# A two-block transformer kernel: one wide matmul for both parts of the tokens in products with stationary weights

## The chip, the cores and the metric

The kernel runs on one core of a Trainium2 chip. The metric is the device time of one execution in microseconds (us); lower is better. The kernel before was timed in three runs.

## The reference, cut to what matters

Two transformer blocks over 256 tokens of width 1024, in fp32. The first has four mixers (gated delta rule, spatial gating, sliding window, memory) on slices of one large input product, each weighted by a gate:

```python
h = _rmsnorm(x, norm_pre)
cols = h @ w_in
...
proj = jnp.einsum("btnc,ncd->btnd", ys, w_up)
gates = jax.nn.sigmoid(gate_logits.reshape(B, T, N_BRANCH, D))
merged = jnp.sum(gates * proj, axis=2)
out = merged @ w_out
return x + _rmsnorm(out, norm_post)
```

The second part has two layers, each with a feed-forward net, an attention (MLA in one, NSA in the other) and a second feed-forward net:

```python
def swiglu(x, w_gate, w_up, w_down):
    return (jax.nn.silu(x @ w_gate) * (x @ w_up)) @ w_down
```

## The kernel before, in words

All large products are made in fp32 accuracy from three products of halves: each operand is split into a part `h` (rounded to the format that TensorE multiplies, fp32r) and a remainder `l`, and `h h + h l + l h` is summed in a PSUM bank. `mm3` (lines 226 to 232) issues these three matmuls; after each it calls `drip`, which issues one or two steps of other work (transposes, attention, the delta rule).

**Weights.** `unit` (lines 192 to 213) brings up to 128 x 2048 numbers by a DMA from SP's queue into `raw` (two buffers) and splits them in two halves of 1024 columns: ACT casts `raw` to `wh` (line 210), DVE subtracts and writes `wl` (line 211). `wh` and `wl` have four buffers each, so units are made some three ahead, and a new unit waits for TensorE to leave the buffer of the fourth before it.

**Tokens.** `xpair` and `ypair` (lines 363 to 371) make the transposed, split tokens: two tiles `xTh` and `xTl` (or `yTh`, `yTl`), each of [128, 8 or 4 k tiles, 256 tokens].

**Two kinds of product.** In one kind (`Product`, line 240) the tokens are stationary and 512 columns of weights stream past. In the other, `ws` (lines 289 to 301), a 128 x 128 block of weights is stationary and the 256 tokens stream; the result has channels on the partitions. `ws` walks over blocks of 128 channels (`j`); two blocks share a bank of `acc` (two banks), and `evac` is called once per bank with 512 columns:

```python
pv = acc().rearrange("p (j t) -> p j t", j=2)
for j in range(2):
    js = slice(j1 + j * P, j1 + (j + 1) * P)
    for k in range(nk):
        ...
        mm3(pv[:, j, :], h[:, k, js], l[:, k, js], xh, xl, k == 0, k == nk - 1)
evac((j0 + j1) // P, 2, pv)
```

So one pair (block, k tile) costs three weight loads and three matmuls of 256 columns. `ws` makes, with 8 k tiles: the three parts of the convolution's input (`convolve`, line 568, whose copy of the bank at line 575 has a raised priority), the gates of two branches (`z_ws`), `qs`, `xq` and `mkT` (lines 846 to 936), the merge gates (line 1006), the queries of NSA (line 1479), and in each of the four feed-forward nets the gate and up products of `hidden` (lines 1078 to 1091), one unit of 256 channels at a time, 18 units per net. With 4 k tiles it makes the up-projections `w_up` of the merge (line 1020), 8 units of 512 channels.

Evacuation reads the bank directly: `silu2` is a tanh on ACT (line 413) and a combining operation on DVE (line 414); `ev_u` (lines 1084 to 1087) multiplies on DVE, casts on ACT and subtracts on DVE; in the merge, DVE weighs the bank by the gate and adds it (lines 1015, 1016).

**Order of the work.** The program's order gives priorities; a scheduler at build time puts each engine's instructions into one fixed sequence. ACT and DVE work through theirs in order, so whatever stands behind a waiting instruction waits too.

Of the kernel before, what the change touches and what calls it, by code (L numbers as in the profile page):

```python
# [14 lines left out]
OP = mybir.AluOpType  # L15
# [12 lines left out]
# how many steps later, beside large products, transposes of fresh rows are issued  # L28
# [4 lines left out]
def _const_table(names):  # L33
    """Constants of the shapes alone, [128, n], with the column range of each."""
# [59 lines left out]
def two_blocks_kernel(ctx: ExitStack, tc: tile.TileContext, a, cst_dram, cst2_dram, out):  # L94
# [120 lines left out]
    def units(W, r0, nk, c0, n, far=False):  # L215
        """The weights of a product by units of k tiles: [[(h, l) of a k tile], ..]; far: two k tiles stand
        for four blocks of 64 rows, the first and third, then the second and fourth."""
# [15 lines left out]

    def block(x, k, t):
        """(h, l) of k tile k of token tile t; x = [(h, l) of up to 4 or 8 k tiles, ..]"""
        nb = x[0][0].shape[1]
        h, l = x[k // nb]
        return h[:, k % nb, t * P:(t + 1) * P], l[:, k % nb, t * P:(t + 1) * P]

    class Product:  # L240
        """out[token, c0:c0+n] of a token tile; segs cuts n into banks; evac(t, segment, bank)."""
# [7 lines left out]
        def run(self, t, u):  # L249
            """unit u for token tile t"""  # L250
# [16 lines left out]
    def in_turns(steps, lead=3, await_second=True):  # L267
        """Units of weights for both token tiles: the first tile runs `lead` units ahead.
        steps = [(product, unit), ..]"""
# [12 lines left out]
    def ts(x, nk, W, r0, c0, n, evac, ps_of=acc):  # L282
        """out[token, n] for each token tile"""
# [5 lines left out]
    def ws(x, nk, W, r0, c0, n, evac):  # L289
        """out[channel, token], two blocks of 128 channels to a bank."""  # L290
        w = 512 if nk <= 4 else 256
        for j0 in range(0, n, w):
            h, l = unit(W, r0, nk, c0 + j0, w)
            for j1 in range(0, w, 256):
                pv = acc().rearrange("p (j t) -> p j t", j=2)
                for j in range(2):
                    js = slice(j1 + j * P, j1 + (j + 1) * P)
                    for k in range(nk):
                        xh, xl = (v[:, k % v.shape[1], :] for v in x[k // x[0][0].shape[1]])
                        mm3(pv[:, j, :], h[:, k, js], l[:, k, js], xh, xl, k == 0, k == nk - 1)  # L300
                evac((j0 + j1) // P, 2, pv)
# [12 lines left out]
    def rstd2(ss, eps):  # L314
        """1/sqrt(mean square + eps) from the two halves of it"""
# [5 lines left out]
    def rstd_of(src, eps):  # L321
        """1/sqrt(mean square + eps) of rows of D"""
# [5 lines left out]
    def transposes(src, n, after, m=P):  # L328
        """n transposes into one bank (m rows each), and what follows of them."""
# [11 lines left out]
    def split_T(src, nb, dst, t, col0=0, wait=None):  # L341
        """Transpose [token, nb*128] into k tiles col0.. of dst = [(h, l), ..], four to a bank; at once,
        or between the next matrix products, from the one that `wait` says."""
# [19 lines left out]
    def xpair():  # L363
        h = per.tile([P, 8, T], F32R, name="xTh", bufs=1)
        l = per.tile([P, 8, T], F32R, name="xTl", bufs=1)
        return [(h, l)]

    def ypair():
        h = per.tile([P, 4, T], F32R, name="yTh", bufs=2)
        l = per.tile([P, 4, T], F32R, name="yTl", bufs=2)  # L370
        return (h, l)
# [16 lines left out]
    class Normed:  # L388
        """The transposed rmsnorm of the residual, a token tile at a time."""
# [14 lines left out]
    def silu2(dst, ps, ph):  # L404
        """2*silu(ps)"""
# [10 lines left out]
    def gelu2(dst, src, ph, w=512):  # L416
        """2*gelu(src), the tanh form"""
# [43 lines left out]
    # =====================================================================  # L461
    # first block
    # =====================================================================
    def first(nxt):
# [36 lines left out]
        def z_ws(name, c0):  # L501
            """2*silu(z) by channels, to be multiplied into"""
            z = ph.tile([P, 4, T], F32, name="y_" + name)
            y[name] = z
            ws(xT, 8, w_in, 0, c0, 512, lambda j0, w, pv: silu2(z[:, j0:j0 + w, :], pv, ph))

        # the gate of the first branch, then beta and the decays
# [60 lines left out]
        def convolve(c):  # L568
            dst = v2 if c == 2 else qk[:, 4 * c:4 * c + 4]

            def ev(j0, w, pv):
                xpad = pc.tile([P, 2, T + 3], F32, name="xpad")
                gp.memset(xpad[:, :, 0:3], 0.0)
                with tc.high_priority(offset=400):
                    sc.copy(xpad[:, :, 3:3 + T], pv)
# [11 lines left out]
            ws(xT, 8, w_in, 0, 512 * c, 512, ev)  # L587

        def norms(c, j0):
            """The sums of squares (and four times the guard) of two heads."""  # L590
# [15 lines left out]
        # [queries or keys, token tile, head]  # L606
# [49 lines left out]
        def deltanet():  # L656
# [20 lines left out]
            for t in range(2):  # L677
# [12 lines left out]
                # inverse of the unit lower triangle by block doubling: Dm and its transpose Em  # L690
# [140 lines left out]
        # keys for the even and the odd head of a pair, zeros in the other's half  # L831
# [14 lines left out]
        ws(xT, 8, w_in, 0, 3592, 512, lambda j0, w, pv: sc.copy(qs[:, j0:j0 + w, :], pv))  # L846
# [17 lines left out]
        def scale_rows(p, nh, w, sm):  # L864
            """The probabilities of nh heads over their sums."""
# [5 lines left out]
        def gated(name, t, bank):  # L871
            """2*y by channels: half of 2*silu(z) times the heads"""
# [3 lines left out]
        def sliding_quads():  # L876
# [56 lines left out]
        ws(xT, 8, w_in, 0, 4872, 512,  # L933
           lambda j0, w, pv: sc.activation(xq[:, j0:j0 + w, :], pv, AF.Copy, scale=128.0 ** -0.5))
        w_kv = a["w_mem_kv"][0]
        ws(mT, 8, w_kv, 0, 0, 512, lambda j0, w, pv: sc.copy(mkT[:, j0:j0 + w, :], pv))
# [54 lines left out]
        for at, (br, name) in enumerate([(1, "b"), (2, "c"), (0, "a"), (3, "m")]):  # L991
# [11 lines left out]
            for n in range(2):  # L1003
                gate = pg.tile([P, 4, T], F32, name="gate", bufs=1)
                ws(xT, 8, w_in, 0, 5896 + br * D + n * 512, 512,
                   lambda j0, w, pv, gate=gate: sc.activation(gate[:, j0:j0 + w, :], pv, AF.Tanh, scale=0.5))
# [13 lines left out]
                ws(yT, 4, a["w_up"][0, br], 0, n * 512, 512, ev)  # L1020
# [24 lines left out]
    # =====================================================================  # L1045
    # second block
    # =====================================================================
# [626 lines left out]
```

## Time and profile before

| what | us |
|---|---|
| median of three runs | 1440.2 |
| lowest, highest run | 1439.85, 1445.96 |
| span of the profiled execution | 1438.7 |
| TensorE matmul busy in it | 1412.1 (98%) |
| DVE busy | 874.6 (61%) |
| ACT busy | 687.9 (48%) |

The profiled execution's span runs from the first to the last instruction; of its own time the profile gives this span alone. Matmuls are pipelined: the duration of one reaches from its start to its modelled end and overlaps the next, so a rate is read from starts in the timeline, not from durations. "PEld" is TensorE loading weights.

### The profile page before, as it was taken

To read this page: it belongs to the slowest core of one execution; us is meant where nothing else is said; L and a number is where in the kernel's file an instruction comes from. 1 tells how busy PE (TensorE), PEld (TensorE's weight loads), DVE (VectorE), ACT (ScalarE), POOL (GpSimd) and SP (SyncE) were. 2 spreads that over 40 slices of the span, in tenths; PEclk is the share of its full clock that TensorE was granted. 3 is DMA by queue.
4 is the path that set the end of the run, shared out by engine and by line. 5 is a ranking of instruction groups with operands and counts; after the bars stand their busy time and mean duration, and the time that the engine had idled before them with its cause. 6 is when DMAs were issued, how large, how long until landed. Compare 5 with 4: busy or idle time off the path is not lost.

```text
span 1438.7 us, 23502 instructions
## 1 busy us (share of the span) xinstructions
PE 1412.1 (98%) x9712; PEld 1282.5 (89%) x9712; DVE 874.6 (61%) x1443; ACT 687.9 (48%) x1149; POOL 44.3 (3%) x87
## 2 busy tenths in 40 slices
PE   7999999999999999999999999999999999999998
PEld 6998989999979999887799998999998976799997
DVE  5878675465576554678564546655555666665554
ACT  5646454443354434466453444434345475553432
POOL 1002000000010000110000000000000000000000
PEclk9999999999999999999999999999999999999999
DMA  7425634555546555433567555555565520365551
GB/s 253 148 85 171 219 112 147 173 176 179 176 157 215 198 177 186 154 121 118 166 223 264 189 193 176 201 178 195 183 214 190 144 60 30 132 205 177 194 186 59
DMA packets 172543, 241.90 MB, mean 168 GB/s; under 512 B 5263, under 2 KB 121748, under 8 KB 172308
## 3 DMA queue, kind: packets, MB, share of 16 engines
q1 hardware_dynamic: 172436, 240.40, 50.5%
q8 instruction: 76, 1.25, 0.3%
q14 instruction: 31, 0.25, 0.1%
HBM read 239.31 MB, written 4.22 MB: 169 GB/s over the span
## 4 chain that ended last, share of the span: by engine, by line
PE 90%; DMA 3%; ACT 2%; DVE 2%; POOL 1%; issue 1%; SPq 0%; POOLq 0%; ACTq 0%; DVEq 0%
PE acc L231 20%; PE acc L229 19%; PE acc L227 19%; PE d L227 5%; PE d L229 5%; PE d L231 5%; PE tr L335 4%; ACT wh L210 1%; DMA raw<-in_w_in_dram 1%; PE wo L1507 1%; PE mm L1507 1%; DVE wl L211 1%; PE po L725 1%; PE po L716 1%; DMA raw<-in_ffn_b_w_up_dram 1%
## 5 line engine op out<-in xcount | busy, mean ns | idle before, releaser
L211 DVE TENSOR_TENSOR wl<-raw,wh 128x1024 fp32r<-128x1024 f32 (+5 forms) x434 | 512.7, 1198 | 327.3 <-ACT wh L210 325.5
L210 ACT CAST wh<-raw 128x1024 fp32r<-128x1024 f32 (+5 forms) x434 | 436.3, 1028 | 526.4 <-PE acc L229 292.2
L227 PE MATMUL acc<-xTh,wh 128*128 128x256 f32 x1696 | 483.3, 285 | 0.0
L229 PE MATMUL acc<-xTl,wh 128*128 128x256 f32 x1696 | 483.2, 285 | 0.0
L231 PE MATMUL acc<-xTh,wl 128*128 128x256 f32 x1696 | 482.7, 285 | 0.0
L227 PEld LDWEIGHTS acc<-xTh,wh 128*128 128x128 f32 x1696 | 325.2, 192 | 2.2 <-PE d L231 0.6
L229 PEld LDWEIGHTS acc<-xTl,wh 128*128 128x128 f32 x1696 | 325.2, 192 | 1.4 <-issue 0.2
L231 PEld LDWEIGHTS acc<-xTh,wl 128*128 128x128 f32 x1696 | 325.2, 192 | 0.5 <-issue 0.2
L231 PE MATMUL d<-wh,yTl 128*128 128x512 f32 x352 | 137.7, 391 | 0.0
L227 PE MATMUL d<-wh,yTh 128*128 128x512 f32 x352 | 137.7, 391 | 0.0
L229 PE MATMUL d<-wl,yTh 128*128 128x512 f32 x352 | 137.7, 391 | 0.0
L227 PE MATMUL acc<-wh,xTh 128*128 128x512 f32 (+4 forms) x256 | 97.8, 383 | 0.5 <-ACT xTh L356 0.5
L231 PE MATMUL acc<-wh,xTl 128*128 128x512 f32 (+4 forms) x256 | 96.5, 379 | 0.2 <-DVE xTl L357 0.2
L229 PE MATMUL acc<-wl,xTh 128*128 128x512 f32 (+4 forms) x256 | 96.7, 378 | 0.0
L231 PEld LDWEIGHTS d<-wh,yTl 128*128 128x128 f32 x352 | 66.1, 188 | 14.3
L227 PEld LDWEIGHTS d<-wh,yTh 128*128 128x128 f32 x352 | 66.1, 188 | 13.3
L229 PEld LDWEIGHTS d<-wl,yTh 128*128 128x128 f32 x352 | 66.2, 188 | 13.1
L1085 DVE TENSOR_TENSOR sg<-sg,acc 128x512 f32<-128x512 f32 x36 | 24.7, 687 | 55.5 <-PE acc L231 55.5
L231 PEld LDWEIGHTS acc<-wh,xTl 128*128 128x128 f32 x256 | 49.0, 192 | 8.8 <-DVE xTl L357 0.9
L227 PEld LDWEIGHTS acc<-wh,xTh 128*128 128x128 f32 x256 | 49.1, 192 | 8.5 <-ACT xTh L356 0.9
L229 PEld LDWEIGHTS acc<-wl,xTh 128*128 128x128 f32 x256 | 49.3, 192 | 7.5
L231 PE MATMUL acc<-yTh,wl 128*128 128x256 f32 x160 | 45.5, 284 | 0.0
(442 smaller groups left out, 1753.1 us busy)
## 6 DMA issues: line engine op xcount, KB each, us to landing
raw<-in_w_in_dram SPq DMA_DIRECT2D x37, 1024.0 KB, 4.9
raw<-in_ffn_a_w_gate_dram SPq DMA_DIRECT2D x22, 1024.0 KB, 5.2
raw<-in_ffn_a_w_up_dram SPq DMA_DIRECT2D x22, 1024.0 KB, 5.2
raw<-in_ffn_a_w_down_dram SPq DMA_DIRECT2D x22, 1024.0 KB, 5.0
raw<-in_ffn_b_w_gate_dram SPq DMA_DIRECT2D x22, 1024.0 KB, 5.1
raw<-in_ffn_b_w_up_dram SPq DMA_DIRECT2D x22, 1024.0 KB, 5.1
raw<-in_ffn_b_w_down_dram SPq DMA_DIRECT2D x22, 1024.0 KB, 5.0
raw<-in_w_up_dram SPq DMA_DIRECT2D x8, 1024.0 KB, 5.0
```

Source lines behind the costliest of these rows:

```text
L210: sc.copy(h[:, c], raw[:, c])
L211: ve.tensor_sub(l[:, c], raw[:, c], f32(h[:, c]))
L227: pe.matmul(ps, ah, bh, start=start, stop=False)
L229: pe.matmul(ps, ah, bl, start=False, stop=False)
L231: pe.matmul(ps, al, bh, start=False, stop=stop)
L335: pe.transpose(box[0][:m, b * P:(b + 1) * P], src(b), ident)
L716: pe.matmul(pv[:, h], O[:, h, :], dv[:, h], start=True, stop=True)
L725: pe.matmul(p[:, h * 64:(h + 1) * 64], Em[:, h, :], Vs[t][:, h, :], start=True, stop=True)
L1085: ve.tensor_mul(sg, sg, p)
L1507: pe.matmul(s[:, i, :], qT[half(h), h // 2, tsl], kT[br][half(h), h // 4, 0:w], start=True, stop=True)
```

## The change: one 512-column matmul over both parts

The tokens' two parts become one tile with the part as an inner dimension, so that `h` and `l` of a k tile lie side by side in 512 columns. In `ws`, the matmul with `h` of the weights takes these 512 columns into a whole bank: `wh xh` into the left half, `wh xl` into the right. The matmul with `l` of the weights adds `wl xh` to the left half. A bank now holds one block of 128 channels instead of two. ACT copies the right half out, DVE adds the left half to it, and `evac` then works on that sum in SBUF. The raised priority of the convolution's copy is gone with that copy. The steps of other work per (block, k tile) stay three.

```diff
+    class Pair:
+        def __init__(self, t):
+            self.t = t
+            self.parts = (t[:, :, 0, :], t[:, :, 1, :])
...
+        def both(self, k):
+            return self.t[:, k]
...
-    def ws(x, nk, W, r0, c0, n, evac):
+    def ws(x, nk, W, r0, c0, n, into, evac=None, scale=None):
...
-                pv = acc().rearrange("p (j t) -> p j t", j=2)
+                b = (j0 + j1) // P
+                dst = into(b)
                 for j in range(2):
                     js = slice(j1 + j * P, j1 + (j + 1) * P)
+                    ps = acc()
                     for k in range(nk):
-                        xh, xl = (v[:, k % v.shape[1], :] for v in x[k // x[0][0].shape[1]])
-                        mm3(pv[:, j, :], h[:, k, js], l[:, k, js], xh, xl, k == 0, k == nk - 1)
-                evac((j0 + j1) // P, 2, pv)
+                        pair = x[k // x[0][0].shape[1]]
+                        kk = k % pair[0].shape[1]
+                        for part in ("hl" if k == 0 else "lh"):
+                            if part == "h":
+                                pe.matmul(ps, h[:, k, js], pair.both(kk), start=k == 0, stop=k == nk - 1)
+                                drip()
+                            else:
+                                pe.matmul(ps[:, :T], l[:, k, js], pair[0][:, kk, :], start=False, stop=False)
+                            drip()
+                    d = dst[:, j, :]
+                    if scale is None:
+                        sc.copy(d, ps[:, T:])
+                        ve.tensor_add(d, d, ps[:, :T])
+                    else:
+                        sc.activation(d, ps[:, T:], AF.Copy, scale=scale)
+                        ve.scalar_tensor_tensor(d, ps[:, :T], scale, d, op0=OP.mult, op1=OP.add)
+                if evac:
+                    evac(b, 2, dst)
...
     def xpair():
-        h = per.tile([P, 8, T], F32R, name="xTh", bufs=1)
-        l = per.tile([P, 8, T], F32R, name="xTl", bufs=1)
-        return [(h, l)]
+        return [Pair(per.tile([P, 8, 2, T], F32R, name="xT", bufs=1))]
...
+            def into(j0):
+                xpad = pads[j0] = pc.tile([P, 2, T + 3], F32, name="xpad")
+                gp.memset(xpad[:, :, 0:3], 0.0)
+                return xpad[:, :, 3:3 + T]
...
             def ev(j0, w, pv):
-                xpad = pc.tile([P, 2, T + 3], F32, name="xpad")
-                gp.memset(xpad[:, :, 0:3], 0.0)
-                with tc.high_priority(offset=400):
-                    sc.copy(xpad[:, :, 3:3 + T], pv)
+                xpad = pads.pop(j0)
...
                 ws(xT, 8, w_in, 0, 5896 + br * D + n * 512, 512,
-                   lambda j0, w, pv, gate=gate: sc.activation(gate[:, j0:j0 + w, :], pv, AF.Tanh, scale=0.5))
+                   lambda j0, gate=gate: gate[:, j0:j0 + 2, :],
+                   lambda j0, w, pv: sc.activation(pv, pv, AF.Tanh, scale=0.5))
...
-                ws(yT, 4, a["w_up"][0, br], 0, n * 512, 512, ev)
+                ws(yT, 4, a["w_up"][0, br], 0, n * 512, 512,
+                   lambda j0: ph.tile([P, 512], F32, name="th", bufs=2).rearrange("p (j t) -> p j t", j=2), ev)
...
-                ws(xT, 8, wg, 0, c0 + j0, 256, lambda j, w, p, sg=sg: silu2(sg, p, pf))
-                ws(xT, 8, wu, 0, c0 + j0, 256, ev_u)
+                ws(xT, 8, wg, 0, c0 + j0, 256, lambda j, sg=sg: sg, lambda j, w, p: silu2(p, p, pf))
+                ws(xT, 8, wu, 0, c0 + j0, 256, lambda j: pf.tile([P, 2, T], F32, name="up", bufs=2), ev_u)
```

The other calls (`z_ws`, `qs`, `xq`, `mkT`, the queries) get the tile to write in the same way; where they only copied or scaled the bank, that copy is now `ws`'s own.

## Rows read from the trace of the kernel before

**Rows 1.** The page: busy time by engine, and the chain that ended last.

```profile
PE 1412.1 (98%) x9712; PEld 1282.5 (89%) x9712; DVE 874.6 (61%) x1443; ACT 687.9 (48%) x1149; POOL 44.3 (3%) x87
...
PE 90%; DMA 3%; ACT 2%; DVE 2%; POOL 1%; issue 1%; SPq 0%; POOLq 0%; ACTq 0%; DVEq 0%
```

**Rows 2.** Groups by line: the first matmul of each triple, 8 and 4 k tiles.

```profile
L227 PE MATMUL acc<-xTh,wh 128*128 128x256 f32 x1696 | 483.3, 285 | 0.0
...
L227 PE MATMUL acc<-yTh,wh 128*128 128x256 f32 x160 | 45.3, 283 | 0.0
```

**Rows 3.** TensorE's timeline (start, duration): a unit's first matmul, and the next unit's.

```profile
484.30 0.28 PE L227 MATMUL acc<-xTh,wh 128*128 128x256 f32 x1
...
490.06 0.40 PE L227 MATMUL d<-wh,yTh 128*128 128x512 f32 x1
```

**Rows 4.** TensorE's timeline: a run of 512-column matmuls, then 256-column ones.

```profile
715.79 0.39 PE L227 MATMUL acc<-wh,xTh 128*128 128x512 f32 x1
...
723.72 0.39 PE L231 MATMUL acc<-wh,xTl 128*128 128x512 f32 x1
723.95 0.28 PE L227 MATMUL acc<-xTh,wh 128*128 128x256 f32 x1
724.06 0.28 PE L229 MATMUL acc<-xTl,wh 128*128 128x256 f32 x1
```

**Rows 5.** Groups by line and shape (busy us, mean ns) of ACT and DVE.

```profile
L211 DVE TENSOR_TENSOR wl<-raw,wh 128x1024 fp32r<-128x1024 f32 x406 | 489.9, 1223 | 319.9 <-ACT wh L210 318.3 <-PE tr L335 1.4
...
L210 ACT CAST wh<-raw 128x1024 fp32r<-128x1024 f32 x406 | 416.3, 1047 | 510.6 <-PE acc L229 289.0 <-PE d L231 103.1 <-PE acc L231 29.1
...
L414 DVE SCALAR_TENSOR_TENSOR sg<-th,acc 128x512 f32<-128x512 f32 x44 | 30.0, 681 | 2.5 <-ACT th L413 2.5
...
L1085 DVE TENSOR_TENSOR sg<-sg,acc 128x512 f32<-128x512 f32 x36 | 24.7, 687 | 55.5 <-PE acc L231 55.5
...
L1015 DVE SCALAR_TENSOR_TENSOR gate<-gate,acc 128x512 f32<-128x512 f32 x12 | 8.2, 683 | 3.9 <-PE acc L231 3.9
...
L727 DVE TENSOR_TENSOR Dm<-Dm,po 128x256 f32<-128x256 f32 x12 | 5.1, 422 | 7.1 <-PE po L725 7.1
...
L719 ACT COPY Vc<-po 128x256 f32<-128x256 f32 x12 | 4.5, 371 | 4.3 <-PE po L716 4.3
...
L575 ACT COPY xpad<-acc 128x512 f32<-128x512 f32 x6 | 3.5, 588 | 7.7 <-PE acc L231 7.7
```

**Rows 6.** ACT's timeline at the end of a gate unit of a feed-forward net.

```profile
484.42 1.05 ACT L210 CAST wh<-raw 128x1024 fp32r<-128x1024 f32 x1 [3.28 <-PE acc L229]
485.37 0.59 ACT L413 ACTIVATE th<-acc 128x512 f32<-128x512 f32 x1
485.86 1.04 ACT L210 CAST wh<-raw 128x1024 fp32r<-128x1024 f32 x1
```

**Rows 7.** All engines' timeline: an up unit's last matmul, and who reads the bank.

```profile
489.94 0.28 PE L231 MATMUL acc<-xTh,wl 128*128 128x256 f32 x1
...
490.25 0.69 DVE L1085 TENSOR_TENSOR sg<-sg,acc 128x512 f32<-128x512 f32 x1 [1.80 <-PE acc L231]
```

**Rows 8.** DVE's timeline in a `w_up` unit of the merge.

```profile
294.11 1.22 DVE L211 TENSOR_TENSOR wl<-raw,wh 128x1024 fp32r<-128x1024 f32 x1 [0.21 <-ACT wh L210]
295.25 0.68 DVE L1015 SCALAR_TENSOR_TENSOR gate<-gate,acc 128x512 f32<-128x512 f32 x1
295.97 0.69 DVE L1016 TENSOR_TENSOR merged<-merged,gate 128x512 f32<-128x512 f32 x1
```

**Rows 9.** Busy time by stretch: merge, convolution, a feed-forward net; TensorE, loads, DVE, ACT, POOL, clock, DMA.

```profile
250.00:390.00 140.00, 140.00 (x1148) 139.05 (x1148) 81.54 (x85) 59.98 (x72) 0.00 (x0) 1.00 0.52 173
36.00:100.00 64.00, 63.55 (x511) 61.38 (x510) 51.05 (x101) 36.24 (x68) 2.61 (x6) 1.00 0.33 107
418.00:600.00 182.00, 182.00 (x1226) 168.67 (x1226) 102.35 (x108) 79.13 (x97) 1.39 (x4) 1.00 0.56 187
```

More of the change, by code (lines that the diff above doesn't have):

```diff
@@ L232, in mm3, with __getitem__, __iter__ @@
         drip()
+    class Pair:
+        def __init__(self, t):
+            self.t = t
+            self.parts = (t[:, :, 0, :], t[:, :, 1, :])
+        def __getitem__(self, i):
+            return self.parts[i]
+        def __iter__(self):
+            return iter(self.parts)
+        def both(self, k):
+            return self.t[:, k]
     def block(x, k, t):
@@ L363, in xpair @@
     def xpair():
-        h = per.tile([P, 8, T], F32R, name="xTh", bufs=1)
-        l = per.tile([P, 8, T], F32R, name="xTl", bufs=1)
-        return [(h, l)]
+        return [Pair(per.tile([P, 8, 2, T], F32R, name="xT", bufs=1))]
     def ypair():
-        h = per.tile([P, 4, T], F32R, name="yTh", bufs=2)
-        l = per.tile([P, 4, T], F32R, name="yTl", bufs=2)
-        return (h, l)
+        return Pair(per.tile([P, 4, 2, T], F32R, name="yT", bufs=2))
     def gain(ap1d, n=D):
@@ L504, in z_ws @@
             y[name] = z
-            ws(xT, 8, w_in, 0, c0, 512, lambda j0, w, pv: silu2(z[:, j0:j0 + w, :], pv, ph))
+            ws(xT, 8, w_in, 0, c0, 512, lambda j0: z[:, j0:j0 + 2, :], lambda j0, w, pv: silu2(pv, pv, ph))
         bl = ph.tile([P, 2, 8], F32)
@@ L569, in convolve @@
             dst = v2 if c == 2 else qk[:, 4 * c:4 * c + 4]
+            pads = {}
+            def into(j0):
+                xpad = pads[j0] = pc.tile([P, 2, T + 3], F32, name="xpad")
+                gp.memset(xpad[:, :, 0:3], 0.0)
+                return xpad[:, :, 3:3 + T]
             def ev(j0, w, pv):
-                xpad = pc.tile([P, 2, T + 3], F32, name="xpad")
-                gp.memset(xpad[:, :, 0:3], 0.0)
-                with tc.high_priority(offset=400):
-                    sc.copy(xpad[:, :, 3:3 + T], pv)
+                xpad = pads.pop(j0)
                 for j in range(2):
@@ L585, in ev @@
                     norms(c, j0)
-            ws(xT, 8, w_in, 0, 512 * c, 512, ev)
+            ws(xT, 8, w_in, 0, 512 * c, 512, into, ev)
         def norms(c, j0):
@@ L845, in first @@
         norm_T(memx[:, 0, :], g2, mT, 0, 40)
-        ws(xT, 8, w_in, 0, 3592, 512, lambda j0, w, pv: sc.copy(qs[:, j0:j0 + w, :], pv))
+        ws(xT, 8, w_in, 0, 3592, 512, into=lambda j0: qs[:, j0:j0 + 2, :])
         norm_T(memx[:, 1, :], g2, mT, 1, 16)
@@ L931, in first @@
         launch(sliding)
-        ws(xT, 8, w_in, 0, 4872, 512,
-           lambda j0, w, pv: sc.activation(xq[:, j0:j0 + w, :], pv, AF.Copy, scale=128.0 ** -0.5))
+        ws(xT, 8, w_in, 0, 4872, 512, lambda j0: xq[:, j0:j0 + 2, :], scale=128.0 ** -0.5)
         w_kv = a["w_mem_kv"][0]
-        ws(mT, 8, w_kv, 0, 0, 512, lambda j0, w, pv: sc.copy(mkT[:, j0:j0 + w, :], pv))
+        ws(mT, 8, w_kv, 0, 0, 512, into=lambda j0: mkT[:, j0:j0 + 2, :])
         ts(mT, 8, w_kv, 0, 512, 512, lambda t, p: sc.copy(mv[:, t, :], p))
@@ L1477, in queries @@
         def queries(c):
-            ws(xT, 8, w_in, 0, 512 * c, 512,
-               lambda j0, w, pv: sc.activation(qT[:, 4 * c + j0:4 * c + j0 + w, :], pv, AF.Copy, scale=-0.125))
+            ws(xT, 8, w_in, 0, 512 * c, 512, lambda j0: qT[:, 4 * c + j0:4 * c + j0 + 2, :], scale=-0.125)
         queries(0)
```

## The prediction

> **What bounds the kernel now.** I read the page first. TensorE's matmuls cover 98% of the span and hold 90% of the chain that ended last; DVE is at 61%, ACT at 48% [rows 1]. So time is gained only where TensorE needs fewer nanoseconds, and lost only where TensorE is made to wait. Next, the groups by line: the triples of `ws` come 1696 times with 8 k tiles and 160 times with 4 [rows 2], 1856 in all. Their durations (285 ns) overlap, so the rate comes from starts in TensorE's timeline: a unit of 48 matmuls of 256 columns takes 484.30 to 490.06, 0.1200 us each [rows 3]; 36 matmuls of 512 columns take 715.79 to 723.95, 0.2267 us each [rows 4]. The second has 256 columns more and takes 0.1067 us more. So a column costs 0.417 ns, at the full clock (1.00 in every stretch [rows 9]), and each matmul with its load carries some 0.0133 us that don't depend on its columns. Last, the stretches: TensorE never stands in the merge and in a feed-forward net, and DVE there is busy 58% and 56%, in the convolution 80% [rows 9].
>
> **TensorE's part.** Per triple, three matmuls of 0.1200 (0.3600 us) become one of 0.2267 and one of 0.1200 (0.3467 us): the columns stay 768, one fixed share of 0.0133 us goes. Times 1856, that is **-24.7 us**. The alternation of lengths is seen only singly: 512 to 256 starts 0.23 after, 256 to 256 then 0.11 to 0.12 [rows 4], and 256 to 512 starts 490.06 - 489.94 = 0.12 after [rows 3, 7]. Each matmul kept its own price, so I take the full gain; the bound on the other side is that alternation gives all of it back, 0.
>
> The Trainium skill, page "TensorE: Matmul & The Clock Gate", section "Back-to-back issue gap", gives a gap of N/2.4 + 2.5 ns at the full clock. By that, a matmul less would save 2.5 ns, and the estimate would be 1856 x 2.5 ns = 4.6 us instead of 24.7. The rows show 13.3 ns.
>
> **The new evacuations.** The 1696 triples make 212 blocks of 8; the 160 are 32 of `mkT` (4 blocks) and 128 of `w_up` (32 blocks): 248 blocks. Each adds an ACT copy of 128x256 out of PSUM (0.371 us) and a DVE addition that reads PSUM (0.422 us) [rows 5]: +92 us on ACT, +105 us on DVE. Sixteen plain ACT copies of whole banks go (0.588 us each [rows 5], -9 us). ACT goes to some 770 us, DVE to 980 us, of about 1426: 54% and 69%. Neither becomes the bound on average; what follows (tanh, products) reads SBUF instead of PSUM, which I cost at nothing. The question is when a bank comes free.
>
> **The deadline of a bank.** Before, a bank held two blocks, 5.76 us of matmuls, and the other bank's reader had that long. Now a bank holds one block of 8 x 0.3467 = 2.77 us (1.39 us with 4 k tiles). The bank of a block whose last matmul starts at 0 is wanted again at 0.23 + 2.77 = 3.00. That matmul ends at 0.39 [rows 4], the reader starts 0.03 later (490.25 after 489.94 + 0.28 [rows 7]), copy and addition take 0.37 + 0.42 with 0.03 between: done at 1.24. So 1.76 us of queueing are allowed.
>
> *Feed-forward nets, 72 units.* A unit is two blocks, and at its end ACT and DVE also split the unit that takes its buffer: ACT's next cast starts 0.95 after one, DVE's next subtraction 1.14 after [rows 6, 8]. Since the last matmul of a block is now the one with `h`, the cast is released together with the copy, not before it as now (484.42, ahead of the tanh at 485.37 [rows 6]); the copy is earlier in the program and I expect it first. Then: copy 0.42, cast 0.79, tanh, cast 2.3 to 3.3; DVE: addition 0.82 to 1.24, subtraction 1.9, silu 3.0 (0.68 [rows 5]), subtraction 3.7 to 4.8. The next block ends at 2.77 + 0.39: its copy runs about 3.3 to 3.7, its addition, behind both subtractions, 4.8 to 5.3. That bank is wanted at 0.23 + 5.55 = 5.78. It fits by half a microsecond, in an up unit (0.687 for the product [rows 5]) by about the same. Cost taken: **0**, with 0 and the 1.2 us per unit of the last rival below as its ends; the cover is that half microsecond, and without it each 0.1 us is 7.2 us over 72 units.
>
> *Merge, 8 units of `w_up`.* Four blocks of 1.39 us, and DVE already ran subtraction, weighing and addition without a gap (294.11, 295.25, 295.97 [rows 8]). From the unit's start: ACT copies the gate's last block at 0.2, casts 0.6, tanh 1.5, copies block 0 at 2.1, casts 2.4, copies block 1 at 3.4. DVE: addition 0.6, subtraction 1.55 to 2.69, addition of block 0 to 3.11; block 2 wants that bank at 2.77: 0.4 us lost. Subtraction 3.4 to 4.55, addition of block 1 to 4.97; block 3 wants it at 4.5: 0.45 lost. Weighing and merging (0.68 + 0.69) hold block 2's addition to 6.7, wanted at 6.4: 0.35 lost. Together 1.2 us, times 8: **+9.6 us**. From below 0 (the scheduler puts additions first), from above twice that (every addition behind a full subtraction, 4 x 0.6).
>
> *Convolution, 6 units.* DVE is at 80% there [rows 9] and gets 6 x 0.84 = 5 us more; its copy loses its raised priority and can stand behind the casts. Taken **+1 us**, bounds 0 and 5. The gates' and queries' units elsewhere have the deadlines of the feed-forward nets: 0.
>
> *Edits with one answer.* SP's queue carries the same DMAs; `raw` comes free up to 0.8 us later, behind the addition, and the ring of four units covers that. POOL's six memsets of `xpad` move ahead of the matmuls; nobody waits. The merge's single `gate` tile is now written from the first block on, 2.8 us earlier, and its last reader ends before. At the end of a net, the last hidden unit is ready 0.9 us later, under the 24 matmuls (5.4 us) of the unit held back for that.
>
> **Sum:** -24.7 + 9.6 + 1.0 = -14.1 us. The profiled span is 1438.7, 1.5 under the median; the change is set against the median: 1440.2 - 14.1 = **1426**. A measurement of this kernel can tell some 0.5%, 7.2 us, from no change.
>
> **Rivals.**
> *All banks in time:* additions always go ahead of subtractions; -24.7, **1416**. For it: weight units are three ahead, so a subtraction can wait. Against: DVE took the subtraction before the weighing [rows 8]. Chance 0.18.
> *Waits in the nets too:* the half microsecond of cover is not there, 0.2 us lost per unit, 72 x 0.2 = 14 us: **1440**, no change. For it: an addition behind both subtractions has 0.5 us left. Chance 0.20.
> *Alternation gives the share back:* if the 0.0133 us belong to changing streams and come back where 512 and 256 alternate, nothing is gained and 10.6 stay: **1451**. Against: rows 3, 4 and 7 show the single changes free. Chance 0.05. The gap rule of the Trainium skill named above goes the same way: with 4.6 us gained it would make 1446.
> *Weight splitting ahead of the evacuation, the slower side:* if ACT's fixed order has both casts before the copy at a unit's end, the copy starts at 0.42 + 2 x 0.95 = 2.3, the addition after both subtractions (1.5, 2.6) at 3.8, done 4.2 against 3.0: 1.2 us per unit. In every second of 72 units that is 43 us: **1469**. It outweighs the gain from 0.2 us per unit on, and is slower by over 0.5% from 0.3 us. Against: today an evacuation goes between the two casts [rows 6]. Chance 0.09.
>
> **How the numbers follow.** The forecast keeps 0.48; its own range is 1419 to 1433 (the merge's wait from 3 to 16 us). Faster: 0.48 + 0.18 = 0.66; same: 0.20; slower: 0.05 + 0.09 = 0.14. The range 1413.5 to 1444 takes in the forecast, the first rival and most of the second; some 0.18 lies outside.
>
> **What would show it.** Right: TensorE's matmuls fall by 1856 to about 7856; in the nets starts go 0.23, 0.12 in turn and a unit takes 5.55 us; in `w_up` gaps of some tenths stand before the third and fourth block, released by DVE's addition. Wrong: a pair of matmuls at 0.36 us (alternation); gaps at block changes in the nets, released by DVE (late banks), with casts ahead of the copy in ACT's timeline (the slower rival); no gaps in the merge (the first).

## The result: 1453.1 us, slower, and the profile after

The changed kernel took 1453.14 us (median of 4 runs, 1447.93 to 1457.59) against 1440.79 beside it: ratio 1.0083, 95% interval 1.0062 to 1.0103. It is slower by 0.8%, and above the predicted range. The profiled execution took 1452.39 us, its span is 1450.6 against 1438.7: **+11.9 us**.

The page of the changed kernel: busy time, granted clock by slice, the chain that ended last.

```profile
PE 1414.0 (97%) x7856; PEld 1189.9 (82%) x7856; DVE 962.7 (66%) x1691; ACT 759.5 (52%) x1381; POOL 44.3 (3%) x87
...
PEclk9979999999999999999999999999999899999999
...
PE 80%; DVE 7%; DMA 6%; ACT 4%; issue 1%; POOL 1%; SPq 0%; POOLq 0%; ACTq 0%; DVEq 0%
```

Beside [rows 1]: 1856 matmuls are gone, as they should be, yet TensorE is busy as long as before. DVE and ACT came close to what was foreseen (963 and 760 us for 980 and 770). Two slices of the clock row stand below 9, and TensorE's share of the chain fell from 90% to 80%.

The costliest groups of the changed kernel, by line and shape.

```profile
L323 PE MATMUL acc<-xT,wh 128*128 128x512 f32 x1696 | 595.2, 400 | 4.1 <-DVE up L331 1.5
...
L326 PE MATMUL acc<-xT,wl 128*128 128x256 f32 x1696 | 446.6, 283 | 0.0
...
L330 ACT COPY sg<-acc 128x256 f32<-128x256 f32 x72 | 26.9, 373 | 88.3 <-PE acc L323 87.7
...
L331 DVE TENSOR_TENSOR sg<-sg,acc 128x256 f32<-128x256 f32 x72 | 29.9, 416 | 52.5 <-ACT sg L330 52.5
```

The new copy takes 0.373 us and the addition 0.416, as [rows 5] had it from other lines (0.371, 0.422).

**Where the time went.** The same instructions stand in both traces, so their times can be laid side by side. Each column is a kernel's time less the time before, in us, in its profiled execution; e4, e9 and e11 are experiments told below. The first line stands early in the convolution, with two of its twelve blocks done. In the kernel before, TensorE's first transposes begin later than in the others (9.46 us, 7.97 to 9.31 there), and e1 and e6, which have nothing wide there, already read -1.7 and -1.6. So this is not the wide matmul's. It is the start of that one execution or the new layout, which all the others share; e6 below cannot tell 1.6 us in its times, so this stays open. Further down it has a row of its own.

| the instruction, and its time before | changed | e4, no additions | e9, none in the convolution | e11, parts left narrow |
|---|---|---|---|---|
| ACT's first copy into `V`, 36.2 | -1.4 | -1.2 | -1.2 | -1.4 |
| ACT's last copy into `V`, L748, 113.8 | +9.4 | -2.3 | -2.3 | -1.5 |
| DVE's first `y_m`, L874, 247.1 | +10.6 | -2.1 | -1.8 | -2.0 |
| DVE's first `merged`, L1034, 400.2 | +11.7 | -6.0 | -0.9 | -5.0 |
| last addition of the first net to `res`, L1106, 597.8 | +10.2 | -9.0 | -2.6 | -8.0 |
| the same of the second net, 891.1 | +7.8 | -12.0 | -5.3 | -10.1 |
| the same of the third net, 1079.3 | +5.3 | -15.0 | -8.3 | -13.1 |
| last addition of the last mixer to `res`, L1157, 1243.4 | +13.5 | -14.8 | -1.0 | -13.1 |
| the same of the fourth net, 1432.1 | +11.9 | -17.8 | -2.5 | -16.1 |

The four nets gain (-1.5, -2.4, -2.5, -1.6). The loss stands in two places: before 114 us, and in the last mixer (+8.2).

**The first place: 68 to 88 us.** Busy time by stretch of the changed kernel (time, then TensorE, loads, DVE, ACT, POOL, granted clock, DMA share, GB/s):

```profile
70.00:74.00 4.00, 2.05 (x14) 1.73 (x15) 3.80 (x7) 0.37 (x1) 0.00 (x0) 0.80 0.00 0
74.00:88.00 14.00, 14.00 (x67) 13.84 (x67) 5.97 (x12) 2.29 (x5) 0.00 (x0) 0.50 0.23 75
```

The same stretches of the kernel before:

```profile
70.00:74.00 4.00, 4.00 (x35) 3.96 (x35) 3.53 (x8) 0.31 (x1) 0.00 (x0) 1.00 0.01 4
74.00:88.00 14.00, 14.00 (x115) 13.35 (x115) 11.00 (x21) 5.99 (x14) 0.00 (x0) 1.00 0.00 1
```

TensorE is busy in all 14 us of the second stretch in both; but it runs 67 matmuls there for 115, at a clock of 0.50, which is 1.2 GHz instead of 2.4. Ahead of that it stood for half of the stretch from 70 to 74. TensorE's timeline of the changed kernel (start, duration; in brackets the idle time and its releaser) shows what was missing:

```profile
68.76 0.39 PE L323 MATMUL acc<-xT,wh 128*128 128x512 f32 x1
71.09 1.11 PE L751 MATMUL po<-Dm,Ob 128*128 128x64 f32 x8 [1.94 <-DVE Ob L747]
72.04 0.69 PE L370 MATMUL tr<-cst,Em 128*128 128x128 f32 x4
...
75.36 3.62 PE L760 MATMUL po<-Vc,Em 128*128 128x64 f32 x16
...
87.16 0.56 PE L326 MATMUL acc<-xT,wl 128*128 128x256 f32 x1
```

Sixteen of the same small products in the kernel before, at full clock:

```profile
77.00 1.95 PE L725 MATMUL po<-Vc,Em 128*128 128x64 f32 x16
```

After 68.76 the next large matmul comes 18.4 us later. Only the delta rule's small products are left, and the first of them wait for DVE; before, large matmuls filled the gaps between them, and none of the gaps was longer than 3.7 us from 64 to 88. The large matmuls are missing because their weights are. DVE's groups from 36 to 70 us, changed kernel:

```profile
L211 DVE TENSOR_TENSOR wl<-raw,wh 128x1024 fp32r<-128x1024 f32 x7 | 8.5, 1217 | 0.5 <-ACT wh L210 0.5
L331 DVE TENSOR_TENSOR xpad<-xpad,acc 128x256 f32<-128x256 f32 x9 | 3.7, 412 | 0.0
```

And the kernel before, same stretch:

```profile
L211 DVE TENSOR_TENSOR wl<-raw,wh 128x1024 fp32r<-128x1024 f32 x9 | 11.2, 1264 | 1.3 <-ACT wh L210 1.3
```

Nine additions took the place of two weight subtractions. From the start to 64 us, 19 half units of weights are split instead of 21; then DVE's order has the delta rule's own chain, and the next subtraction comes at 79.7:

```profile
79.74 1.22 DVE L211 TENSOR_TENSOR wl<-raw,wh 128x1024 fp32r<-128x1024 f32 x1
```

It makes the second half of the convolution's last unit. At 68.76 the two blocks of that unit are half done, four of eight k tiles each, and hold both banks; the 8 triples that are left (2.8 us at 0.350) need this half. The next product, whose large matmuls begin at 73.49 in the kernel before, begins at 106.97. So TensorE lacks a weight here and not a bank. Nor is DVE short of time by then: it is busy for 5.97 of the 14 us from 74 on. The subtraction is late by its place in DVE's fixed order.

**The second place: the last mixer.** TensorE's timeline of the changed kernel there:

```profile
1137.83 0.46 PE L1499 MATMUL mm<-hid,w2k 128*128 128x128 f32 x2 [0.75 <-issue]
1138.56 0.47 PE L323 MATMUL acc<-xT,wh 128*128 128x512 f32 x1 [0.28 <-DVE qT L334]
...
1140.55 6.88 PE L1484 MATMUL wo<-flat,w 128*128 128x60 f32 x32 [1.40 <-DMA w<-in_nsa_cmp_w_v_dram]
```

The same 32 products before:

```profile
1136.55 3.78 PE L1448 MATMUL wo<-flat,w 128*128 128x60 f32 x32 [0.28 <-DMA w<-in_nsa_cmp_w_v_dram]
```

They take 6.88 us for 3.78: half clock again, after the waits of 0.75, 0.28 and 1.40 us shown. The weight `w` of the values takes the buffer of the keys' weight, so its transfer is issued only after the last product of the keys (0.36 us after, in both traces), and from there to the first use 6.8 us pass (7.5 before). Before, 54 matmuls of the queries stood between the two in TensorE's order, 6.5 us of work at 0.120; now 21 do, 3.7 us of work at 0.350 us for two; the others stand behind.

By the granted clock, the two stretches lasted 17.1 and 10.2 us; taking half of that as lost, an estimate that the 3.62 us for 1.95 and the 6.88 for 3.78 bear out, they cost 8.5 + 5.1 = **13.6 us**. The kernel before has no such stretch in its profile. (The last 4 to 6 us of every profile, that of the kernel before too, stand at 0.50 as well and are left out in this document.) Some of its other executions lose clock too, as the last section tells.

### The profile page after: what moved, and what is told of

Same layout as the page of the kernel before. It is cut to its first block, busy times and chain, and to the rows that moved or that the text cites. A ratio compares the mean times of both kernels' runs of the same rounds, so it can differ in the third digit from the quotient of the medians.

```text
span 1450.6 us, 20134 instructions
## 1 busy us (share of the span) xinstructions
PE 1414.0 (97%) x7856; PEld 1189.9 (82%) x7856; DVE 962.7 (66%) x1691; ACT 759.5 (52%) x1381; POOL 44.3 (3%) x87
## 4 chain that ended last, share of the span: by engine, by line
PE 80%; DVE 7%; DMA 6%; ACT 4%; issue 1%; POOL 1%; SPq 0%; POOLq 0%; ACTq 0%; DVEq 0%
PE acc L323 25%; PE acc L326 12%; PE d L231 6%; PE d L227 6%; PE d L229 6%; PE tr L370 4%; DVE wl L211 4%; PE acc L231 3%; PE acc L229 3%; PE acc L227 3%; ACT wh L210 3%; PE po L760 1%; PE po L751 1%; PE mm L1542 1%; PE wo L1542 1%
## 5 line engine op out<-in xcount | busy, mean ns | idle before, releaser
L323 PE MATMUL acc<-xT,wh 128*128 128x512 f32 x1696 | 595.2, 400 | 4.1 <-DVE up L331 1.5
L326 PE MATMUL acc<-xT,wl 128*128 128x256 f32 x1696 | 446.6, 283 | 0.0
L323 PEld LDWEIGHTS acc<-xT,wh 128*128 128x128 f32 x1696 | 307.8, 188 | 64.1 <-DVE up L331 2.8
L326 PEld LDWEIGHTS acc<-xT,wl 128*128 128x128 f32 x1696 | 321.0, 189 | 18.7 <-issue 1.0
L231 PE MATMUL d<-wh,yT 128*128 128x512 f32 x352 | 138.0, 392 | 0.0
L227 PE MATMUL d<-wh,yT 128*128 128x512 f32 x352 | 137.7, 391 | 0.0
L229 PE MATMUL d<-wl,yT 128*128 128x512 f32 x352 | 137.5, 391 | 0.0
L227 PE MATMUL acc<-wh,xT 128*128 128x512 f32 (+4 forms) x256 | 97.4, 381 | 0.3 <-ACT xT L391 0.3
L229 PE MATMUL acc<-wl,xT 128*128 128x512 f32 (+4 forms) x256 | 96.3, 376 | 0.0
L231 PE MATMUL acc<-wh,xT 128*128 128x512 f32 (+4 forms) x256 | 96.2, 378 | 0.0
L231 PEld LDWEIGHTS d<-wh,yT 128*128 128x128 f32 x352 | 66.1, 188 | 15.0 <-DVE yT L1123 0.8
L227 PEld LDWEIGHTS d<-wh,yT 128*128 128x128 f32 x352 | 66.1, 188 | 13.1
L331 DVE TENSOR_TENSOR sg<-sg,acc 128x256 f32<-128x256 f32 x72 | 29.9, 416 | 52.5 <-ACT sg L330 52.5
L323 PE MATMUL acc<-yT,wh 128*128 128x512 f32 x160 | 59.6, 408 | 1.4 <-DVE th L331 1.0
L331 DVE TENSOR_TENSOR up<-up,acc 128x256 f32<-128x256 f32 x72 | 29.9, 416 | 41.9 <-ACT up L330 41.9
L227 PEld LDWEIGHTS acc<-wh,xT 128*128 128x128 f32 x256 | 48.8, 191 | 8.5 <-ACT xT L391 0.7
L231 PEld LDWEIGHTS acc<-wh,xT 128*128 128x128 f32 x256 | 48.7, 191 | 8.6 <-DVE xT L392 0.6
```

The source lines that it names most:

```text
L227: pe.matmul(ps, ah, bh, start=start, stop=False)
L229: pe.matmul(ps, ah, bl, start=False, stop=False)
L231: pe.matmul(ps, al, bh, start=False, stop=stop)
L323: pe.matmul(ps, h[:, k, js], pair.both(kk), start=k == 0, stop=k == nk - 1)
L326: pe.matmul(ps[:, :T], l[:, k, js], pair[0][:, kk, :], start=False, stop=False)
L331: ve.tensor_add(d, d, ps[:, :T])
```

## Experiments

In all of them "wide" means the changed form, and "narrow" the `ws` of the kernel before with its three 256-column matmuls and its evacuation, kept beside the new one as `ws3` (its inner lines stand at e6). The theories: the **clock** (additions on DVE make TensorE stand at two places, and the clock then falls to half) and late **banks** (every bank comes free a little late, everywhere).

**e4, the changed kernel without any addition.** ACT copies the left half of the bank; the right half, `wh` by `xl`, is computed and not read. The scaled copy of the queries is changed in the same way.

```
-                        sc.copy(d, ps[:, T:])
-                        ve.tensor_add(d, d, ps[:, :T])
+                        sc.copy(d, ps[:, :T])
```

> The changed kernel without DVE's 248 additions: ACT copies the left half alone, so the product of the weights' h with the tokens' l is computed and left out of the sum. CLOCK with DVE as its cause (additions push the weights' subtractions back where DVE is full): the convolution's matmuls go on between 69 and 87 us, the first half-clock stretch is gone, and the change keeps most of 1856 x 10 ns: 1420 to 1428 us. A rival in which the alternation of widths or the tokens' layout costs the time: still 1445 us or more.

Measured: 1422.17 us, ratio 0.9864 (0.9838 to 0.9890). The groups of its page:

```profile
PE 1393.5 (98%) x7856; PEld 1178.7 (83%) x7856; DVE 875.9 (62%) x1443; ACT 760.4 (54%) x1381; POOL 43.5 (3%) x87
...
PEclk9999999999999999999999999999999999999999
...
L323 PE MATMUL acc<-xT,wh 128*128 128x512 f32 x1696 | 591.1, 398 | 0.8 <-DVE y_b L453 0.8
```

The matmuls alone are worth 17.9 us by the medians (1440.1 beside it), 16.6 by the marks from 36.2 on. In the nets it is 3.0 us each, 12.0 for 1152 triples, 10.4 ns a triple; in the merge 3.9 for 384, 10.2 ns; the other 320, in stretches where TensorE also waits for other engines, bring 0.7 us. Copies on ACT and a bank for each block, which that copy now frees, cost nothing that shows: the waits of L323 for DVE's additions are gone, and so are both stretches of half clock. All that makes the change slow, 1453.1 - 1422.2 = 31 us, hangs on DVE's additions: on their time there, or on the bank that each holds until it is done.

**e6, the new layout of the tokens with narrow matmuls everywhere.**

```
+    def ws3(x, nk, W, r0, c0, n, evac):
...
+                    for k in range(nk):
+                        xh, xl = (v[:, k % v.shape[1], :] for v in x[k // x[0][0].shape[1]])
+                        mm3(pv[:, j, :], h[:, k, js], l[:, k, js], xh, xl, k == 0, k == nk - 1)
+                evac((j0 + j1) // P, 2, pv)
...
-            ws(xT, 8, w_in, 0, c0, 512, lambda j0: z[:, j0:j0 + 2, :], lambda j0, w, pv: silu2(pv, pv, ph))
+            ws3(xT, 8, w_in, 0, c0, 512, lambda j0, w, pv: silu2(z[:, j0:j0 + w, :], pv, ph))
```

(and so at every call)

> The tokens' two parts side by side in one tile as in the change, but all of ws with three narrow matmuls and direct evacuations as before. Both theories: the layout alone does nothing, 1440 us within 0.3%. If it were the cause: above 1445 us.

Measured: 1440.43 us, ratio 0.9997 (0.9978 to 1.0016). The layout does nothing that shows; the interval leaves some 3 us to either side.

**e2, the changed kernel with a narrow convolution.**

```
-            ws(xT, 8, w_in, 0, 512 * c, 512, into, ev)
+            ws3(xT, 8, w_in, 0, 512 * c, 512, ev)
```

> The changed kernel with the convolution's six units (48 banks' worth of 8 triples each, 96 triples) as before. CLOCK: the first stretch at half clock goes, with 8.5 us of clock and some 3 us of waiting: 1442 us, clock about 0.996. BANKS: 5% of the loss goes: 1452 us.

Measured: 1438.45 us, ratio 0.9985 (0.9968 to 1.0002). By 64 us 21 halves are split again, and the stretch of half clock at 72 us is gone; the last copy into `V` is 1.6 us earlier than before, all of it from the start. The stretch of 10.2 us in the last mixer stays, and one of 3.4 us at 185 us, whose cause I did not trace. It came out below both expectations: six units give back some 15 us. (Their 96 triples are 12 banks' worth, not 48.)

**e3, convolution and the last mixer's queries narrow.**

```
-            ws(xT, 8, w_in, 0, 512 * c, 512, lambda j0: qT[:, 4 * c + j0:4 * c + j0 + 2, :], scale=-0.125)
+            ws3(xT, 8, w_in, 0, 512 * c, 512,
+                lambda j0, w, pv: sc.activation(qT[:, 4 * c + j0:4 * c + j0 + w, :], pv, AF.Copy, scale=-0.125))
```

> The changed kernel with the convolution and the NSA queries as before. CLOCK: both stretches go, 8.5 + 5.1 us of clock and some 5 us of waiting: 1434 us, clock 0.999. BANKS: 9% of the loss goes: 1452 us.

Measured: 1429.22 us, ratio 0.9921 (0.9900 to 0.9942). Ten units of `ws` have now been taken out of the change, and it is 24 us faster for it, 5 us below the expectation. The profiled execution (1434.36) still had half clock for 3.4 us at 186 and for 10.2 us from 1196.7, in the attention of the last mixer; the others ran at 0.995 to 1.00.

**e5, the convolution's weights with raised priority,** all else as changed.

```
+            with tc.high_priority(offset=early) if early else ExitStack():
+                h, l = unit(W, r0, nk, c0 + j0, w)
...
-            ws(xT, 8, w_in, 0, 512 * c, 512, into, ev)
+            ws(xT, 8, w_in, 0, 512 * c, 512, into, ev, early=400)
```

> The changed kernel; in the convolution alone, the making of a weight unit (its DMA, casts and subtractions) gets a raised priority, so that DVE's subtractions stand ahead of its additions and filters. Theory STARVED (DVE, over its measure there, makes weights late, so TensorE has only the delta rule's short matmuls for 17 us, waits between them, and its clock halves): large matmuls stand between the delta rule's from 69 to 87 us again, the first stretch at half clock goes, 1442 us as with the convolution undone at best, 1447 at worst. Rival BANKS: late banks, not late weights, hold the convolution's matmuls: additions now come later still, 1453 us or more.

Measured: 1450.86 us, ratio 1.0073 (1.0048 to 1.0098). A miss: the time lies between the two expectations. By 70 us 23 halves are split, but the next comes at 97.4, and the large matmuls stop at 77.2 for 12.5 us. The lack of weights moved to a later place, with 6.8 us of half clock from 81.1 and 3.4 from 46.9; the new order is also 4.7 us late by the first mark of the table. At DVE's first `y_c` (200.0 us before) this kernel is 11.1 us late, the changed one 11.3. To put the weights first does not take the work off DVE; it only changes what comes late.

**e9, no additions in the convolution alone.** This tells DVE's load from all else that is new there.

```
-                        sc.copy(d, ps[:, T:])
-                        ve.tensor_add(d, d, ps[:, :T])
+                        sc.copy(d, ps[:, T:] if add else ps[:, :T])
+                        if add:
+                            add.tensor_add(d, d, ps[:, :T])
...
-            ws(xT, 8, w_in, 0, 512 * c, 512, into, ev)
+            ws(xT, 8, w_in, 0, 512 * c, 512, into, ev, add=None)
```

> The changed kernel, but in the convolution's three products the left half of the bank is copied out by ACT and nothing is added (the part of those products in xh and wl and xh and wh stays, that in xl and wh is left out): 12 DVE additions of 0.42 us fewer, every copy, bank and matmul as in the changed kernel. Theory DVE LOAD (5 us of additions in the stretch where DVE is full delay its weight subtractions, TensorE runs out of weights and its clock is halved): the 17 us of half clock at 72 us go, from 66 to 120 us the kernel is no longer than before, total 1438 to 1442. Rival BANKS OR ACT (one bank per block, or the copy behind the casts on ACT, starves TensorE): the stretch stays, total 1449 or more.

Measured: 1438.27 us, ratio 0.9992 (0.9982 to 1.0002). Its stretches, then DVE's group of weights from 36 to 70 us:

```profile
70.00:74.00 4.00, 4.00 (x27) 3.57 (x26) 3.59 (x8) 1.78 (x4) 0.00 (x0) 1.00 0.00 0
74.00:88.00 14.00, 14.00 (x120) 13.50 (x118) 10.47 (x21) 4.53 (x10) 0.00 (x0) 1.00 0.14 43
```

```profile
L211 DVE TENSOR_TENSOR wl<-raw,wh 128x1024 fp32r<-128x1024 f32 x9 | 11.0, 1217 | 0.1
```

Nine subtractions again, 120 matmuls in the second stretch, full clock. Twelve additions, 5 us of DVE, cost the changed kernel 14.9 us by the medians; by the marks 12.4 of it is lost by 247.1. The additions on DVE are shown to be the cause of the first place; the copy on ACT, which e9 keeps, is not. e9 also frees each bank one addition sooner, so by itself it does not tell a late bank from a late weight; the changed kernel's trace does, with both banks half filled at 68.76. In the last mixer 21 matmuls still stand between the keys' and the values' products, TensorE waits 1.88 us for `w`, and 6.8 us of half clock remain.

**e10, no additions in the last mixer's queries alone.** The scaled copy in `ws` takes `add` as the plain one does in e9.

```
-            ws(xT, 8, w_in, 0, 512 * c, 512, lambda j0: qT[:, 4 * c + j0:4 * c + j0 + 2, :], scale=-0.125)
+            ws(xT, 8, w_in, 0, 512 * c, 512, lambda j0: qT[:, 4 * c + j0:4 * c + j0 + 2, :], scale=-0.125, add=None)
```

> The changed kernel, but the 8 blocks of the last mixer's queries are copied out by ACT with their scale and nothing is added (their part in xl and wh is left out): 8 DVE additions fewer, all else as in the changed kernel. Theory LATE QUERIES (the additions on DVE hold up queries and banks, TensorE idles by turns and is at half clock from 1140 us): that stretch goes, the one at 72 us stays, total 1444 to 1447. Rival ORDER OF THE COMPRESSION (TensorE waits there for a weight's transfer and for the hidden part of the compression, whatever the queries do): the stretch stays, total 1451 to 1454.

Measured: 1444.14 us, ratio 1.0035 (1.0018 to 1.0052). TensorE's timeline at the values' products:

```profile
1135.93 3.78 PE L1486 MATMUL wo<-flat,w 128*128 128x60 f32 x32
```

There are 38 matmuls between the keys' and the values' products instead of 21, 6.6 us of work, no wait for `w`, full clock. So the additions shifted the order around that transfer. The time agrees with the expectation, but only in part for its reason: another stretch of half clock, 10.2 us from 1203.6, came in the attention, and the first one was shorter in this execution (6.8 us).

**e1, wide in the nets alone.**

```
-                ws(xT, 8, w_in, 0, 5896 + br * D + n * 512, 512,
+                ws3(xT, 8, w_in, 0, 5896 + br * D + n * 512, 512,
...
-                ws(yT, 4, a["w_up"][0, br], 0, n * 512, 512,
+                ws3(yT, 4, a["w_up"][0, br], 0, n * 512, 512, ev)
```

(and so at every other place but the nets; the expectation's 2.3 us is 2.5 by the marks)

> The wide matmul only in the four feed-forward nets (1152 of the 1856 triples); the convolution, gates, queries and up-projections have three narrow ones again. Theory CLOCK (the loss is two stretches of 17.1 and 10.2 us at half clock, begun where the convolution's and the NSA queries' products run short): no half clock, and the nets keep the 8 us that the stages of the changed kernel show there (1.5 + 2.4 + 2.3 + 1.6): 1433 us. Rival BANKS (each block's bank comes late everywhere, and the 12.4 us are spread over all triples): 62% of the loss stays, 1448 us.

Measured: 1429.13 us, ratio 0.9914 (0.9896 to 0.9932), no stretch of half clock. The nets gave 9.9 us by the marks, where e4 gives 12.0. The banks come free in time there, but for at most some 2 us over 72 units if that difference is theirs.

**e7, nets and the merge's gates wide.**

```
-                ws3(xT, 8, w_in, 0, 5896 + br * D + n * 512, 512,
+                ws(xT, 8, w_in, 0, 5896 + br * D + n * 512, 512,
```

(against e1: the gates as in the changed kernel, all other places as in e1)

> The wide matmul in the nets (1429.1 us alone) and in the merge's gates (256 triples of 8 k tiles, one block 2.8 us), but not in the up-projections (blocks of 1.4 us), nor before. If only the short blocks of the up-projections lose time in the merge: 256 x 10 ns = 2.6 us less, 1426.5 us. If the merge's additions cost wherever they stand: 1429 to 1431 us.

Measured: 1429.03 us, ratio 0.9907 (0.9883 to 0.9932). The gates gave 3.0 us by the marks at 247.1 and 400.2 in the profiled execution (1426.13, clock 0.999), but four of six ran at 0.994 to 0.995, at 1428 to 1430. Median against median it is no faster than e1: inconclusive.

**e8, e1 with the two lengths grouped** in a block: one wide matmul, eight narrow, seven wide.

```
-                    for k in range(nk):
+                    for k, part in [(0, "h")] + [(k, "l") for k in range(nk)] + [(k, "h") for k in range(1, nk)]:
```

> The wide matmul in the nets alone (1429.1 us), in another order: per block one 512-column matmul, then the eight of 256 columns, then seven of 512. If the 0.350 us per triple measured (0.233 + 0.117) instead of 0.3467 come from alternating widths: starts go to 0.227 and 0.120, 1152 x 3.3 ns = 3.8 us less, 1425.3 us. If not: 0.233 stays between 512-column matmuls, 1429 us.

Measured: 1428.68 us, ratio 0.9920 (0.9894 to 0.9946). A wide matmul starts 231 ns before the next (median), a narrow one 120: 351 ns for a triple; in turns it is 350. Two of its six runs, 1432.0 and 1434.8 us, ran at 0.994 to 0.995. The alternation is not what keeps the gain at 10 ns.

**e11, all wide but the convolution, the last mixer's queries and `w_up`.**

```
-            ws(xT, 8, w_in, 0, 512 * c, 512, into, ev)
+            ws3(xT, 8, w_in, 0, 512 * c, 512, ev)
...
-                ws(yT, 4, a["w_up"][0, br], 0, n * 512, 512,
+                ws3(yT, 4, a["w_up"][0, br], 0, n * 512, 512, ev)
```

(and the queries as in e3)

> The changed kernel with the narrow matmuls of the kernel before in the convolution, the last mixer's queries and w_up; wide ones in the gates, the branches' gates z, the window's and memory's queries, the memory's keys and the nets. 1500 of 1856 triples or so remain wide at 10 ns each. Theory COVER (a wide product costs nothing where DVE has room): 1424 to 1426 at full clock, 5 below the version with the nets alone wide. Rival CLOCK ANYWHERE (half-clock stretches come back in the merge or after it, as soon as more than the nets is wide): 1429 or more.

Measured: 1425.46 us (1424.41 to 1426.04), ratio 0.9901 (0.9886 to 0.9915). Its page:

```profile
PE 1395.7 (98%) x8144; PEld 1194.4 (84%) x8144; DVE 944.5 (66%) x1639; ACT 749.2 (53%) x1339; POOL 44.1 (3%) x87
...
PEclk9999999999999999999999999999999999999999
```

1568 triples are wide (9712 - 8144); 14.5 us were measured, 9.3 ns for each. It beats the kernel before by 1.0% and the changed one by 1.9%.

## Why the prediction was wrong

The terms, and what the runs showed in their place. TensorE's part is e4's column of the table of marks from 36.2 to the end; the other terms are the changed kernel's column less that of e4, which does the same matmuls and copies and adds nothing, from mark to mark.

| step of the prediction | predicted | shown |
|---|---|---|
| the start, to 36.2 | 0 | -1.4 |
| TensorE's part | -24.7 | -16.6 |
| convolution, 6 units | +1.0, bounds 0 and 5 | +11.9 to 114 us, 8.5 of it half clock |
| the stretch up to the merge | 0 | +1.0 |
| merge, 8 units of `w_up` | +9.6 | +5.0 |
| nets, 72 units | 0 | +4.0 |
| gates' and queries' units elsewhere | 0 | +8.0 in the last mixer, 5.1 of it half clock |
| sum | -14.1 | +11.9 |

**The step that failed first** is the convolution: "DVE is at 80% there [rows 9] and gets 6 x 0.84 = 5 us more", taken at +1 and at most 5. The 5 us of DVE work were right. Wrong was the bound: it held that work on DVE can cost at most its own length. It cost 11.9 us, because what it pushed back in DVE's order was a weight that TensorE was to run beside the delta rule (the trace, at 79.74), and because TensorE then ran its small products at half clock (the trace); without these additions both are gone (e9). [Rows 9] showed DVE at 51 of 64 us; the question that was not put is which of DVE's works is the last that TensorE has in hand, and how much of it is ready (the first rival trusted in units made three ahead; two halves fewer were enough).

**The second** is the sentence that queries "elsewhere have the deadlines of the feed-forward nets: 0". A deadline was worked out for the bank, not for the work beside it. In the last mixer TensorE's order weaves the queries with products whose weight is in transfer; the additions moved the weave. Wide and narrow together, 21 matmuls (3.7 us) came to cover the 6.8 us of its transfer, where 38 (6.6 us) do without additions (e10), and TensorE waited.

**No rival named the clock.** All of them priced a wait at its own length. The waits ahead of the lower clock are short, 1.94 us and three of 0.28 to 1.40; the half clock that followed cost 8.5 and 5.1. The Trainium skill, page "TensorE: Matmul & The Clock Gate", section "HAM oscillation — how this bites in real kernels", tells of waits for a transfer after which the next products run at the lower clock. The trace agrees at 1140.55, with 6.88 us for 3.78.

**TensorE's part** had the right mechanism and the wrong size. "Each matmul kept its own price" does not hold: a wide matmul starts 233 ns before the next instead of 226.7, and a narrow one 117 instead of 120.0 (medians of the changed kernel). TensorE's timeline of the changed kernel in a gate of the merge:

```profile
292.57 0.40 PE L323 MATMUL acc<-xT,wh 128*128 128x512 f32 x1
292.81 0.28 PE L326 MATMUL acc<-xT,wl 128*128 128x256 f32 x1
292.92 0.40 PE L323 MATMUL acc<-xT,wh 128*128 128x512 f32 x1
...
295.72 0.40 PE L323 MATMUL acc<-xT,wh 128*128 128x512 f32 x1
```

Nine triples take 3.15 us, 0.350 each, not 0.3467: 10 ns less than 0.3600. Where TensorE sets the pace that is what e4 shows (10.4 and 10.2 ns); for 320 of the 1856 triples even this hardly reaches the end. The 226.7 was read from matmuls with tokens stationary [rows 4]; why the same length costs 6 ns more with weights stationary is open (e8 rules out the alternation). The gap rule of the Trainium skill that the prediction weighed (same page, section "Back-to-back issue gap") would give 2.5 ns a triple, as an estimate: the section gives the rule for a matmul by itself. The 10.4 ns of e4 in the nets speak against it here, though they are less than the 13.3 that I took.

**The merge** went as the prediction described it, more seldom. TensorE's loads waiting between 247 and 400 us, grouped:

```profile
PEld acc L323 <- DVE th L331: 5.8, 14, 0.5
```

And one of the 14, in the timeline of all engines:

```profile
287.78 0.39 ACT L330 COPY th<-acc 128x256 f32<-128x256 f32 x1
...
287.92 1.22 DVE L211 TENSOR_TENSOR wl<-raw,wh 128x1024 fp32r<-128x1024 f32 x1 [0.18 <-ACT wh L210]
...
289.06 0.41 DVE L331 TENSOR_TENSOR th<-th,acc 128x256 f32<-128x256 f32 x1
...
289.53 0.19 PEld L323 LDWEIGHTS acc<-yT,wh 128*128 128x128 f32 x1 [0.39 <-DVE th L331]
```

The copy is done at 288.17, the subtraction holds DVE until 289.14, the addition follows, and the next block's load waits 0.39 us: the "0.4 us lost" of the prediction. There are 14 such waits of 0.41 us, where three for each of 8 units were counted.

**The nets** held their cover: 4.0 us over 72 units, 0.06 each, where the rival "Waits in the nets too" needed 0.2. That rival, "Alternation gives the share back" (0.350, not 0.36 us) and "Weight splitting ahead of the evacuation" (the nets gain) all fell, and so did "All banks in time" (the merge waits). The result was slower for a reason that none of them held; that the 1451 of the alternation lies near the measured 1453 is chance.

## What to carry to other kernels

Where an engine off the critical path prepares operands for the one on it, work added to it is not bounded by its own length: ask how many prepared units stand between it and a gap, and what TensorE runs in that gap. Where the profile shows a full clock everywhere, price a wait twice, once as it is and once with the small products after it at half rate. A change to a helper with many callers is worth trying caller by caller: here six units of one caller cost some 15 us, and without three callers the same change gains 1.0%.

## What the hardware showed that I had not expected

The clock falls while TensorE is still given work. In the stretch from 70 to 74 us it was busy for 2.05 us of 4 and the clock fell within it; from 74 to 88, with TensorE busy throughout at 67 matmuls for 115, it stayed at 0.50.

The clock also explains the spread of the changed kernel. Its four runs took 1452.39, 1457.59, 1453.88 and 1447.93 us at mean clocks of 0.990, 0.986, 0.989 and 0.993. Less the lost share of the span, (1 - clock) x span, they are 1437.9, 1437.2, 1437.9 and 1437.8. So nearly all of their spread is time at half clock, and at full clock the change would, by this estimate, be about even with the kernel before. Then the additions still cost some 16 us in waits (29.9 us of the terms above, less 13.6), as much as the matmuls gain.

The kernel before is not free of it. Of its 53 executions beside the experiments, 10 ran at mean clocks of 0.991 to 0.995 and took 1443.7 to 1451.1 us; the others ran at 0.998 to 1.000 and took 1438.4 to 1441.3. e6, all narrow, has two such runs in ten, at 0.995. So some of the clock is lost without any wide matmul or addition; where, no profile shows, since those that were kept of these two kernels ran at 0.999. The four runs of the changed kernel, at 0.986 to 0.993, each lose more than nine of these ten.
